# Graph message passing by counting matmuls: 384-column segments with a spill zone, no head chunks, one-hots of 32 chunks

## The chip, the cores and the metric

The kernel runs on one core of one Trainium2 chip. The metric is the device time of one execution in microseconds (us), given as the median of repeated executions. Engines are named as in the profile: PE is TensorE's matmuls, PEld its weight loads, DVE is VectorE, ACT is ScalarE, POOL is GpSimd, SP the engine that only issues DMAs. L360 means line 360 of the kernel that the line belongs to; line numbers differ between kernels, so a helper that issues many matmuls has one line (L359 before, L360 after, is the helper that issues counts, heads and clears).

## The reference

```python
N, E, D = 4096, 262144, 256
def reference(nodes, edges_src, edges_dst, w_msg, w_self):
    self_out = nodes @ w_self
    msg = nodes[edges_src] @ w_msg
    agg = np.zeros((N, D)); np.add.at(agg, edges_dst, msg)
    return self_out + agg
```

The kernel never gathers rows. It sorts the 262144 edges, and then builds, for each block of 128 source nodes and each segment of destination nodes, a matrix of counts ("how many edges go from this source to that destination"). The messages of a segment are then count matrix times Y, where Y = nodes @ w_msg. The counts are made by TensorE: a chunk of 128 sorted edges becomes two one-hot matrices, e_oh (edge x source within the block) and d_oh (edge x destination, relative to a base, 96 wide), and one matmul of the two adds the counts of the chunk to a PSUM bank at an address read from a register.

## The kernel before

The sort is the same in both kernels. After it come 2048 chunks. A run is one (segment, source block) pair: 8 segments of 512 destinations x 32 blocks = 256 runs of about 8 chunks. Each run has its own PSUM bank in a ring of six. The parts that matter (cut):

```python
SEGW, W, SL, RING, MARG, LAG, NRUN = 512, 96, 16, 6, 10, 14, 256

def onehots(src, rel, tag):                  # two VectorE instructions for SL = 16 chunks
    for nm, val, wid in (("e", src, P), ("d", rel, W)):
        o = ohp.tile([P, SL // 2, wid, 2], BF16, ...)
        tt(out=o[:], in0=val...to_broadcast(shp), in1=jrow..., op=ALU.is_equal)

def head_mm(r, he, hd_):                     # opens the bank of run r
    after = [evac_of[r - RING]] if r >= RING else []
    count_mm(ring[:, b:b + W], he, hd_, r % SL, True, after)

def evac(r):                                 # ACT copies the finished bank to SBUF as bf16
    ins = nc.scalar.copy(out=at[:], in_=ring[:, b:b + SEGW]).ins

def apply_run(r):                            # counts x Y, accumulated over the 32 blocks
    for t in range(SEGW // P):
        nc.tensor.matmul(out=out_ps[:, t, :], lhsT=at[:, t * P:(t + 1) * P], rhs=Y[:, b, :], ...)
    # ... after the last block: ACT copies out_ps to o_sb, a DMA stores it

for c in range(NCOL):
    if c % SL == 0:
        e, d = onehots(slo_b[:, sl_], rel_b[:, sl_], "c")
        # ... one-hots of 16 head chunks when due
    for r in range(NRUN):
        if max(8 * r - MARG, 0) == c:
            head_mm(r, *heads[r // SL])
    # ... address of the chunk from a register
    count_mm(ring[:, bass.ds(off, W)], e, d, ci, False)
    # ... evac(nev) and, LAG chunks later, apply_run
```

A chunk that runs over the end of a segment is counted twice: once for the segment that it starts in, and once as the "head chunk" of the next run. The head matmul also opens the bank. To build the one-hots of the heads the kernel must first find the chunks: sorted keys go to DRAM, a count locates the chunk, an indirect DMA fetches it, a transpose turns it.

## Time and profile before

| | before |
|---|---|
| time, median of 3 runs | 798.29 us |
| DVE busy | 717.2 of 796.2 us |
| sort, until the minima k are reduced | 0 to 473 us |
| counting loop | 501.9 us (first matmul) to the end |

The busy row of the page (engine, busy us, share of the span, instructions):

```profile
PE 353.0 (44%) x3906; PEld 300.8 (38%) x3906; DVE 717.2 (90%) x859; ACT 215.9 (27%) x375; POOL 18.6 (2%) x32
```

A share of the whole span mixes the stages. The table of busy time by window separates them; its columns are the window, its length, and busy us (with the number of instructions) of PE, PEld, DVE, ACT and POOL, then the granted TensorE clock, the DMA share and GB/s:

```profile
20.00:480.00 460.00, 108.53 (x512) 87.70 (x512) 419.43 (x531) 50.56 (x96) 7.35 (x6) 0.77 0.08 18
480.00:500.00 20.00, 0.89 (x2) 0.36 (x2) 7.66 (x25) 4.19 (x4) 2.06 (x2) 0.50 0.05 17
600.00:700.00 100.00, 82.87 (x1168) 72.63 (x1166) 100.00 (x101) 54.43 (x94) 0.00 (x0) 0.98 0.05 18
```

In the loop DVE is busy 100 of 100 us. In the window before it, 480 to 500 us, nearly everything stands still, on the way to the head chunks. The timeline of DVE there, with one line of ACT (start, busy us, engine, line, operation, count, and in brackets the idle time before and what ended it):

```profile
484.04 0.95 DVE L343 TENSOR_TENSOR d_oh<-rel_b,jrow 128x1536 bf16<-128x1536 bf16 x1
485.36 0.19 ACT L292 ACTIVATION_READ_ACCUMULATOR junk<-gball,thr 128x1 f32 x1
492.42 0.28 DVE L484 TENSOR_REDUCE bsum<-brow 1x1 f32<-1x128 f32 x1 [7.42 <-DMA brow<-fd]
492.80 0.15 DVE L296 TENSOR_SCALAR cnt<-cnt 128x2 f32<-128x2 f32 x1
496.76 0.29 DVE L314 CAST hs_i<-xt_ps 128x128 int32<-128x128 f32 x1 [3.61 <-PE xt_ps L313]
499.43 1.23 DVE L343 TENSOR_TENSOR e_oh<-hsl,jrow 128x2048 bf16<-128x2048 bf16 x1
```

The first ordinary d_oh is built at 484 us; the loop gets going at 499 us, when the head chunks have come.

How fast is each engine inside the loop? DVE, two one-hot instructions per 16 chunks:

```profile
655.77 1.22 DVE L343 TENSOR_TENSOR e_oh<-slo_b,jrow 128x2048 bf16<-128x2048 bf16 x1
656.90 0.95 DVE L343 TENSOR_TENSOR d_oh<-rel_b,jrow 128x1536 bf16<-128x1536 bf16 x1
657.77 1.22 DVE L343 TENSOR_TENSOR e_oh<-slo_b,jrow 128x2048 bf16<-128x2048 bf16 x1
```

From start to start a pair takes 2.0 us, although the two durations add up to 2.17: they overlap a little, so starts are the right thing to count. PE, in a stretch where it has caught a backlog and does not wait:

```profile
655.48 0.55 PE L359 MATMUL ring<-d_oh,e_oh 128*128 128x96 bf16 x9
655.88 0.60 PE L401 MATMUL out_ps<-Y,at 128*128 128x256 bf16 x4
656.31 0.56 PE L359 MATMUL ring<-d_oh,e_oh 128*128 128x96 bf16 x9
656.70 0.60 PE L401 MATMUL out_ps<-Y,at 128*128 128x256 bf16 x4
```

Nine counts (8 chunks and a head) start 0.40 us before the four applies, which start 0.43 us before the next counts: 44 ns per count, 108 to 109 per apply, 0.83 us per run. An estimate from the Trainium skill comes close: "TensorE: Matmul & The Clock Gate", section Back-to-back issue gap, gives N/2.4 + 2.5 ns for an isolated warm matmul of N columns, from which I estimate 42.5 ns for 96 and 109 for 256. (That section also says that in a stream with weight loads the spacing differs, about 81 ns at N = 128; this trace does not show that.) So PE needs 256 x 0.83 = 212 us where DVE needs 144 pairs x 2.005 = 289 us (128 of chunks, 16 of heads), and the waits agree that PE waits for DVE:

```profile
PE ring L359 <- DVE d_oh L343: 41.3, 84, 4.0
PE out_ps L396 <- ACT o_sb L408: 5.4, 7, 0.8
```

(waited for: us in total, times, longest).

### The profile page before, as it was taken

To read this page: it belongs to the slowest core of one execution; us is meant where nothing else is said; L and a number is where in the kernel's file an instruction comes from. 1 tells how busy PE (TensorE), PEld (TensorE's weight loads), DVE (VectorE), ACT (ScalarE), POOL (GpSimd) and SP (SyncE) were. 2 spreads that over 40 slices of the span, in tenths; PEclk is the share of its full clock that TensorE was granted. 3 is DMA by queue.
4 is the path that set the end of the run, shared out by engine and by line. 5 is a ranking of instruction groups with operands and counts; after the bars stand their busy time and mean duration, and the time that the engine had idled before them with its cause. 6 is when DMAs were issued, how large, how long until landed. Compare 5 with 4: busy or idle time off the path is not lost. (4 is left out here: it accounts for less than half of the span.)

```text
span 796.2 us, 10040 instructions
## 1 busy us (share of the span) xinstructions
PE 353.0 (44%) x3906; PEld 300.8 (38%) x3906; DVE 717.2 (90%) x859; ACT 215.9 (27%) x375; POOL 18.6 (2%) x32
## 2 busy tenths in 40 slices
PE   0013232003232222332212130788888988878886
PEld 0000000002232222332212130667776877767775
DVE  1999999998989888888898973999999999999994
ACT  1001111001111111111101032345555555545554
POOL 4300000000000000000000001000000000000000
PEclk9999999998666655556656655799999999999999
DMA  6741110000000000000000011000000000000000
GB/s 224 105 118 26 25 26 17 0 0 0 1 0 0 1 0 0 0 0 1 0 0 0 0 60 56 1 2 28 2 28 28 2 28 3 27 2 28 2 28 29
DMA packets 25210, 17.91 MB, mean 22 GB/s; under 512 B 11557, under 2 KB 24358, under 8 KB 24390
## 3 DMA queue, kind: packets, MB, share of 16 engines
q1 hardware_dynamic: 19862, 11.59, 4.8%
q0 software_dynamic: 4720, 2.49, 2.3%
q10 hardware_dynamic: 578, 3.16, 1.0%
q8 instruction: 32, 0.52, 0.3%
q14 instruction: 18, 0.15, 0.1%
HBM read 10.12 MB, written 7.37 MB: 22 GB/s over the span
## 5 line engine op out<-in xcount | busy, mean ns | idle before, releaser
L578 DVE TENSOR_TENSOR XA<-XA 128x1024 f32<-128x1024 f32 (+1 forms) x294 | 262.1, 939 | 16.1 <-ACT XA L559 11.3
L375 ACT CAST at<-ring 128x512 bf16<-128x512 f32 x256 | 149.8, 586 | 146.2 <-PE ring L359 146.0
L359 PE MATMUL ring<-d_oh,e_oh 128*128 128x96 bf16 x2304 | 148.0, 208 | 42.7 <-DVE d_oh L343 41.3
L578 DVE TENSOR_TENSOR XB<-XB 128x256 f32<-128x256 f32 (+1 forms) x196 | 139.9, 764 | 19.9 <-ACT XB L559 16.6
L359 PEld LDWEIGHTS <-e_oh 128*128 128x128 bf16 x2304 | 132.8, 99 | 64.2 <-issue 45.4
L343 DVE TENSOR_TENSOR e_oh<-slo_b,jrow 128x2048 bf16<-128x2048 bf16 x128 | 155.9, 1218 | 0.0
L401 PE MATMUL out_ps<-Y,at 128*128 128x256 bf16 x1024 | 155.9, 275 | 0.0
L343 DVE TENSOR_TENSOR d_oh<-rel_b,jrow 128x1536 bf16<-128x1536 bf16 x128 | 121.7, 951 | 0.0
L556 PE MATMUL tp_sw<-sid,XA 128*128 128x128 f32 x224 | 41.7, 372 | 138.6 <-DVE XA L578 138.6
L556 PEld LDWEIGHTS tp_sw<-sid,XA 128*128 128x128 f32 x224 | 40.6, 285 | 139.8 <-issue 139.8
L556 PE MATMUL tp_sw<-ident,XB 128*128 128x128 f32 x224 | 41.6, 371 | 115.7 <-DVE XB L578 115.7
L401 PEld LDWEIGHTS <-at 128*128 128x128 bf16 x1024 | 87.1, 98 | 7.8 <-ACT at L375 0.6
L556 PEld LDWEIGHTS tp_sw<-ident,XB 128*128 128x128 f32 x224 | 40.4, 284 | 116.8 <-issue 116.8
L207 PE MATMUL y_ps<-wcat,XT 128*128 128x256 bf16 x64 | 25.2, 394 | 107.9 <-DMA XT<-nodes_bf_dram 107.9
L559 ACT COPY XB<-tp_sw 128x512 f32<-128x512 f32 x28 | 16.4, 585 | 164.2 <-PE tp_sw L556 164.2
L207 PEld LDWEIGHTS <-XT 128*128 128x128 bf16 x64 | 6.7, 104 | 126.2 <-DMA XT<-nodes_bf_dram 126.2
L559 ACT COPY XA<-tp_sw 128x512 f32<-128x512 f32 x28 | 16.3, 586 | 138.2 <-PE tp_sw L556 138.2
L211 ACT CAST Y<-y_ps 128x256 bf16<-128x256 f32 x32 | 11.9, 372 | 104.0 <-PE y_ps L207 104.0
L343 DVE TENSOR_TENSOR e_oh<-hsl,jrow 128x2048 bf16<-128x2048 bf16 x16 | 19.5, 1219 | 0.0
L343 DVE TENSOR_TENSOR d_oh<-hrel,jrow 128x1536 bf16<-128x1536 bf16 x16 | 15.2, 951 | 0.0
L308 POOL DMA_INDIRECT xh<-xs_dram,cidx x2 | 2.1, 1028 | 466.4 <-DVE cidx L299 466.1
L313 PE MATMUL xt_ps<-ident,xh 128*128 128x128 f32 x2 | 0.9, 447 | 26.3 <-DMA xh<-xs_dram,cidx 26.3
(87 smaller groups left out, 91.9 us busy)
## 6 DMA issues: line engine op xcount, KB each, us to landing
out_dram<-o_sb SPq DMA_DIRECT2D x16, 256.0 KB, 2.3
s<-in_edges_src_dram ACTq DMA_DIRECT2D x2, 1024.0 KB, 12.5
d<-in_edges_dst_dram SPq DMA_DIRECT2D x2, 1024.0 KB, 10.2
nodes_bf<-in_nodes_dram POOLq DMA_DIRECT2D x1, 2048.0 KB, 16.1
nodes_bf_dram<-nodes_bf SPq DMA_DIRECT2D x1, 2048.0 KB, 9.0
XT<-nodes_bf_dram SPq DMA_TRANSPOSE x64, 2.4
xs_dram<-XA ACTq DMA_DIRECT2D x1, 1024.0 KB
gball<-gd SPq DMA_DIRECT2D x1, 1024.0 KB
```

What stands on the lines that cost most here:

```text
L207: nc.tensor.matmul(out=y_ps[:], lhsT=XT[:, k, t * P:(t + 1) * P], rhs=wcat[:, 2 + k, :], start=(k == 0), stop=(k == 1),)
L211: nc.scalar.copy(out=Y[:, t, :], in_=y_ps[:])
L308: nc.gpsimd.indirect_dma_start(out=xh[:], out_offset=None, in_=xs_dram[:, :], in_offset=bass.IndirectOffsetOnAxis(ap=cidx[:, h:h + 1], axi ...
L313: nc.tensor.transpose(xt_ps[:, 0:P], xh[:], ident[:])
L343: tt(out=o[:], in0=val.rearrange("p (g i) -> p g i", i=2).unsqueeze(2).to_broadcast(shp), in1=jrow[:, 0:wid, :].unsqueeze(1).to_broadcast( ...
L359: mm = nc.tensor.matmul(out=ap, lhsT=e[:, ci // 2, :, ci % 2], rhs=d[:, ci // 2, :, ci % 2], start=start, stop=True, skip_group_check=True ...
L375: ins = nc.scalar.copy(out=at[:], in_=ring[:, b:b + SEGW]).ins
L401: nc.tensor.matmul(out=out_ps[:, t, :], lhsT=at[:, t * P:(t + 1) * P], rhs=Y[:, b, :], start=False, stop=(b == T - 1), skip_group_check=True,)
L556: nc.tensor.matmul(out=tp[:, k * P:(k + 1) * P], lhsT=src[:, c], rhs=rhs[:], start=True, stop=True)
L559: nc.scalar.copy(out=dst[:, q * 512:(q + 1) * 512], in_=tp[:])
L578: nc.vector.tensor_tensor(out=d4[:, :, t, :], in0=s4[:, :, 0, :], in1=hi, op=op)
```

## The change

The intent is to take work from DVE. Segments become 384 columns wide, but keep a bank of 512: a chunk that runs over the end of its segment writes on into a spill zone of 96 columns, and the next run adds that zone with one more apply. So there are no head chunks, no head chain, no head one-hots. One-hots are built 32 chunks at a time. The price: 320 runs of 384 and 32 of 256 columns (352 instead of 256), an additional apply per run, and, as no head matmul opens the bank any more, two clears: matmuls of zeros that open the bank and write zeros over its first 96 columns and its spill zone. (They are needed because, as the Trainium skill says in "PSUM — Partial Sum Buffer", section The four PSUM rules, opening a bank clears the marks of what was written, not the data; columns that no count writes would keep old data.) The core of the diff:

```diff
-SEGW = 512
-SL = 16
-MARG = 10
-LAG = 14
-NRUN = 256
+BW = 512
+SW = 384
+NB = 32
+NBIG = 320
+NRUN = 352
+MARG = 9
+LAG = 12
...
     # keys: segment of 384 instead of a shift by 9
+        nc.vector.scalar_tensor_tensor(out=cut, in0=seg, scalar=29.5, in1=blk, op0=ALU.is_gt, op1=ALU.mult)
+        tss(out=seg, in_=seg, scalar=43, op=ALU.mult)
+        tss(out=seg, in_=seg, scalar=7, op=ALU.logical_shift_right)
-        for v, i in ((dlo, 1), (dhi, 2), (shi, 3)):
+        for v, i in ((dlo, 1), (cut, 4), (seg, 2), (blk, 3)):
...
-    # the head chain: Sign/accumulate, indirect DMA, transposes, hsl, hrel
...
+    sizes = [8, 8, 16] + [32] * ((NCOL - 64) // 32) + [16, 8, 8]
+            o = ohp.tile([P, 16, wid, 2], BF16, name=nm + "_oh", tag=nm, bufs=4)
...
+    zer = ohp.tile([P, 2, P], BF16, name="zer")
+    nc.gpsimd.memset(zer[:], 0.0)
...
+    def clear(r):
+        b = (r % RING) * BW
+        w = width(r)
+        after = [evac_of[r - RING]] if r >= RING else []
+        ap = ring[:, b:b + BW]
+        lo = ap[:, 0:W]
+        hi = ap[:, w:w + W]
+        count_mm(lo, zer[0:1, 0, :], zer[0:1, 1, 0:W], True, after)
+        count_mm(hi, zer[0:1, 0, :], zer[0:1, 1, 0:W], False, after)
...
-    def head_mm(r, he, hd_):
...
     def apply_run(r):
+        if r > 0:
+            w = width(r - 1)
+            m = P if w == SW else W
+            nc.tensor.matmul(
+                out=out_ps[0:m, 0, :], lhsT=at_of.pop(r - 1)[:, w:w + m], rhs=Y[:, b, :],
+                start=False, stop=False, skip_group_check=True,
+            )
```

More of the change, by code (lines that the diff above doesn't have):

```diff
@@ L18 @@
 ACTF = mybir.ActivationFunctionType
-SEGW = 512
+BW = 512
+SW = 384
 W = 96
-SL = 16
+NB = 32
+NBIG = 320
+NRUN = 352
+CBIG = 1920
 RING = 6
-MARG = 10
-LAG = 14
-NRUN = 256
+MARG = 9
+MARG2 = 6
+LAG = 12
 PSUM0 = 0x2000000
@@ L59 @@
     T = N // P
-    NSEG = N // SEGW
     NSTAGE = 18
@@ L70 @@
     nodes_bf_dram = dram.tile([N, D], BF16, name="nodes_bf_dram")
-    xs_dram = dram.tile([NCOL, P], FP32, name="xs_dram")
     kd = dram.tile([1, NCOL + 1], FP32, name="kd")
@@ L75 @@
     fd = dram.tile([1, P], FP32, name="fd")
-    rd = dram.tile([1, NCOL + 64], I32, name="rd")
     ident = const.tile([P, P], FP32, name="ident")
@@ L89 @@
     sgn = const.tile([P, 8], FP32, name="sgn")
-    ksg = const.tile([P, 4], FP32, name="ksg")
+    ksg = const.tile([P, 5], FP32, name="ksg")
     nc.gpsimd.iota(sgi[:], pattern=[[0, 8]], base=0, channel_multiplier=1)
@@ L104 @@
     )
-    for i, m in enumerate((1.0, 128.0, float((1 << 21) - (1 << 16)), float((1 << 16) - P))):
+    for i, m in enumerate((1.0, 128.0, float((SW * (NB - 1)) << 7), float((SW << 7) - P), float(-(1 << 14)))):
         nc.vector.tensor_scalar(
@@ L132 @@
         hi = XB[h][:].bitcast(I32)
-        dhi = hi[:, 0:HC]
-        shi = hi[:, HC:2 * HC]
+        seg = hi[:, 0:HC]
+        blk = hi[:, HC:2 * HC]
         key = XA[0][:, h * HC:(h + 1) * HC]
+        cut = XA[1][:, h * HC:(h + 1) * HC]
         nc.scalar.activation(out=key, in_=slo, func=ACTF.Copy, scale=ksg[:, 0:1])
-        tss(out=dhi, in_=dlo, scalar=9, op=ALU.logical_shift_right)
-        tss(out=shi, in_=slo, scalar=7, op=ALU.logical_shift_right)
-        for v, i in ((dlo, 1), (dhi, 2), (shi, 3)):
+        tss(out=blk, in_=slo, scalar=7, op=ALU.logical_shift_right)
+        tss(out=seg, in_=dlo, scalar=7, op=ALU.logical_shift_right)
+        nc.vector.scalar_tensor_tensor(
+            out=cut, in0=seg, scalar=29.5, in1=blk, op0=ALU.is_gt, op1=ALU.mult
+        )
+        tss(out=seg, in_=seg, scalar=43, op=ALU.mult)
+        tss(out=seg, in_=seg, scalar=7, op=ALU.logical_shift_right)
+        for v, i in ((dlo, 1), (cut, 4), (seg, 2), (blk, 3)):
             nc.vector.scalar_tensor_tensor(
@@ L150 @@
     jrow = const.tile([P, P, 2], BF16, name="jrow")
-    hbase = const.tile([P, NRUN], FP32, name="hbase")
-    thr = const.tile([P, 2], FP32, name="thr")
     lo_c = const.tile([P, G16], I32, name="lo_c")
@@ L160 @@
     nc.gpsimd.tensor_copy(out=jrow[:], in_=jrow_i[:])
-    hb_i = stgn.tile([P, NRUN], I32, name="hb_i")
-    nc.gpsimd.iota(hb_i[:], pattern=[[1, NRUN]], base=0, channel_multiplier=0)
-    nc.gpsimd.tensor_copy(out=hbase[:], in_=hb_i[:])
-    nc.gpsimd.tensor_scalar(
-        out=hbase[:], in0=hbase[:], scalar1=float(SEGW), scalar2=None, op0=ALU.mult
-    )
-    nc.gpsimd.memset(hbase[:, 0:1], float(1 << 17))
-    thr_i = stgn.tile([P, 2], I32, name="thr_i")
-    nc.gpsimd.iota(thr_i[:], pattern=[[P, 2]], base=0, channel_multiplier=1)
@@ L170 @@
-    nc.gpsimd.tensor_copy(out=thr[:], in_=thr_i[:])
-    nc.gpsimd.tensor_scalar(
-        out=thr[:], in0=thr[:], scalar1=float(SEGW), scalar2=-0.5, op0=ALU.mult, op1=ALU.add
-    )
-    c_i = stgn.tile([P, G16], I32, name="c_i")
-    nc.gpsimd.iota(c_i[:], pattern=[[1, G16]], base=-MARG, channel_multiplier=G16)
-    nc.vector.tensor_single_scalar(out=lo_c[:], in_=c_i[:], scalar=3, op=ALU.arith_shift_right)
-    c_j = stgn.tile([P, G16], I32, name="c_j")
-    nc.gpsimd.iota(c_j[:], pattern=[[1, G16]], base=MARG, channel_multiplier=G16)
@@ L179 @@
-    nc.vector.tensor_single_scalar(out=hi_c[:], in_=c_j[:], scalar=3, op=ALU.arith_shift_right)
-    NPER = (NCOL + 64) // 48
-    r_i = stgn.tile([1, NPER * 48], I32, name="r_i")
-    nc.gpsimd.iota(
-        r_i[:].rearrange("p (a b c) -> p a b c", b=RING, c=8),
-        pattern=[[0, NPER], [1, RING], [0, 8]], base=0, channel_multiplier=0,
-    )
-    nc.sync.dma_start(rd[0:1, 0:NPER * 48], r_i[:])
-    lo6 = stgn.tile([P, G16], I32, name="lo6")
-    o6 = 48 - MARG
-    nc.sync.dma_start(lo6[:], rd[0, o6:o6 + NCOL].rearrange("(p g) -> p g", g=G16))
@@ L190, with clamp, muladd @@
-    nc.vector.tensor_tensor(out=lom_c[:], in0=lo_c[:], in1=lo6[:], op=ALU.subtract)
+    c_i = stgn.tile([P, G16], I32, name="c_i")
+    ta = stgn.tile([P, G16], I32, name="ta")
+    tb = stgn.tile([P, G16], I32, name="tb")
+    lo6 = stgn.tile([P, G16], I32, name="lo6")
+    def clamp(out, in_, lo, hi):
+        nc.vector.tensor_scalar(
+            out=out, in0=in_, scalar1=float(lo), scalar2=float(hi), op0=ALU.max, op1=ALU.min
+        )
+    def muladd(out, in_, m, a):
+        nc.vector.tensor_scalar(
+            out=out, in0=in_, scalar1=float(m), scalar2=float(a), op0=ALU.mult, op1=ALU.add
+        )
@@ new lines @@
+    for dst, off, top, off2, top2 in (
+        (lo_c, -MARG, CBIG, -MARG2 - CBIG, NCOL - 1 - CBIG),
+        (hi_c, MARG, CBIG - 1, MARG2 + 4 - CBIG, NCOL - CBIG + 3),
+    ):
+        nc.gpsimd.iota(c_i[:], pattern=[[1, G16]], base=0, channel_multiplier=G16)
+        muladd(ta[:], c_i[:], 1, off)
+        clamp(ta[:], ta[:], 0, top)
+        muladd(ta[:], ta[:], 683, 0)
+        tss(out=ta[:], in_=ta[:], scalar=12, op=ALU.logical_shift_right)
+        muladd(tb[:], c_i[:], 1, off2)
+        clamp(tb[:], tb[:], 0, top2)
+        tss(out=tb[:], in_=tb[:], scalar=2, op=ALU.logical_shift_right)
+        tt(out=dst[:], in0=ta[:], in1=tb[:], op=ALU.add)
@@ L192 @@
+    muladd(lo6[:], lo_c[:], 683, 0)
+    tss(out=lo6[:], in_=lo6[:], scalar=12, op=ALU.logical_shift_right)
+    muladd(lom_c[:], lo6[:], RING, 0)
     nodes_bf = stgn.tile([P, T, D], BF16, name="nodes_bf")
@@ L231 @@
     gn = meta.tile([P, G16], I32, name="gn")
+    qa = meta.tile([P, G16], I32, name="qa")
+    qb = meta.tile([P, G16], I32, name="qb")
     dl = meta.tile([P, G16], I32, name="dl")
-    ex = meta.tile([P, G16], I32, name="ex")
     gb = meta.tile([P, G16], FP32, name="gb")
@@ L239 @@
     poffs = meta.tile([1, NCOL], I32, name="poffs")
-    junk = meta.tile([P, NCOL], BF16, name="junk")
-    cnt = meta.tile([P, 2], FP32, name="cnt")
-    cidx = meta.tile([P, 2], I32, name="cidx")
-    nc.scalar.dma_start(xs_dram.rearrange("(p g) l -> p (g l)", g=G16), srt[:])
     nc.vector.tensor_copy(out=k16i[:], in_=k16[:])
     tss(out=gi[:], in_=k16i[:], scalar=7, op=ALU.logical_shift_right)
-    tss(out=dl[:], in_=gi[:], scalar=SEGW - 1, op=ALU.bitwise_and)
-    nc.vector.tensor_scalar(
-        out=ex[:], in0=dl[:], scalar1=float(W - SEGW), scalar2=0.0, op0=ALU.add, op1=ALU.max
-    )
-    tt(out=gb[:], in0=gi[:], in1=ex[:], op=ALU.subtract)
+    nc.vector.tensor_copy(out=gb[:], in_=gi[:])
     nc.sync.dma_start(gd[0, :].rearrange("(p g) -> p g", g=G16), gb[:])
     nc.sync.dma_start(gball[:], gd[0:1, :].broadcast_to([P, NCOL]))
-    tss(out=rho[:], in_=gi[:], scalar=9, op=ALU.logical_shift_right)
+    tss(out=qa[:], in_=gi[:], scalar=7, op=ALU.logical_shift_right)
+    clamp(qb[:], qa[:], 3 * NBIG, 1 << 16)
+    clamp(qa[:], qa[:], 0, 3 * NBIG)
+    muladd(qa[:], qa[:], 683, 0)
+    tss(out=qa[:], in_=qa[:], scalar=11, op=ALU.logical_shift_right)
+    muladd(qb[:], qb[:], 1, -3 * NBIG)
+    tss(out=qb[:], in_=qb[:], scalar=1, op=ALU.logical_shift_right)
+    tt(out=rho[:], in0=qa[:], in1=qb[:], op=ALU.add)
+    nc.vector.scalar_tensor_tensor(
+        out=dl[:], in0=qa[:], scalar=float(-SW), in1=gi[:], op0=ALU.mult, op1=ALU.add
+    )
+    nc.vector.scalar_tensor_tensor(
+        out=dl[:], in0=qb[:], scalar=-256.0, in1=dl[:], op0=ALU.mult, op1=ALU.add
+    )
     tt(out=rhoc[:], in0=rho[:], in1=lo_c[:], op=ALU.max)
@@ L258 @@
     nc.vector.tensor_scalar(
-        out=wr[:], in0=sl[:], scalar1=float(RING), scalar2=float(-RING * SEGW),
+        out=wr[:], in0=sl[:], scalar1=float(RING), scalar2=float(-RING * BW),
         op0=ALU.is_ge, op1=ALU.mult,
@@ L262 @@
     nc.vector.scalar_tensor_tensor(
-        out=wr[:], in0=sl[:], scalar=float(SEGW), in1=wr[:], op0=ALU.mult, op1=ALU.add
+        out=wr[:], in0=sl[:], scalar=float(BW), in1=wr[:], op0=ALU.mult, op1=ALU.add
     )
-    tt(out=dl[:], in0=dl[:], in1=ex[:], op=ALU.subtract)
     tt(out=poff[:], in0=wr[:], in1=dl[:], op=ALU.add)
@@ L288 @@
         tss(out=ki[:, s], in_=ki[:, s], scalar=7, op=ALU.logical_shift_right)
-    for h in range(2):
-        nc.scalar.activation(
-            out=junk[:], in_=gball[:], func=ACTF.Sign, bias=thr[:, h:h + 1], scale=-1.0,
-            accum_out=cnt[:, h:h + 1],
-        )
-    nc.vector.tensor_scalar(
-        out=cnt[:], in0=cnt[:], scalar1=0.5, scalar2=float(NCOL // 2 - 1), op0=ALU.mult, op1=ALU.add
-    )
-    nc.vector.tensor_scalar(
-        out=cidx[:], in0=cnt[:], scalar1=0.0, scalar2=None, op0=ALU.max
-    )
-    hs_i = meta.tile([P, NRUN], I32, name="hs_i")
-    hd_i = meta.tile([P, NRUN], I32, name="hd_i")
-    hsl = meta.tile([P, NRUN], BF16, name="hsl")
-    hrel = meta.tile([P, NRUN], BF16, name="hrel")
-    for h in range(2):
-        xh = meta.tile([P, P], FP32, name=f"xh{h}")
-        nc.gpsimd.indirect_dma_start(
-            out=xh[:], out_offset=None, in_=xs_dram[:, :],
-            in_offset=bass.IndirectOffsetOnAxis(ap=cidx[:, h:h + 1], axis=0),
-        )
-        xt_ps = psum_sort.tile([P, 512], FP32, name="xt_ps", tag="tp", bufs=4)
-        nc.tensor.transpose(xt_ps[:, 0:P], xh[:], ident[:])
-        nc.vector.tensor_copy(out=hs_i[:, h * P:(h + 1) * P], in_=xt_ps[:, 0:P])
-    tss(out=hd_i[:], in_=hs_i[:], scalar=7, op=ALU.logical_shift_right)
-    tss(out=hs_i[:], in_=hs_i[:], scalar=P - 1, op=ALU.bitwise_and)
-    nc.vector.tensor_copy(out=hsl[:], in_=hs_i[:])
-    tt(out=hrel[:], in0=hd_i[:], in1=hbase[:], op=ALU.subtract)
     psum_sort.release()
@@ L330, with onehots @@
     psum2 = tc.alloc_tile_pool(name="psum2", bufs=1, space=bass.MemoryType.PSUM)
-    ring = psum2.tile([P, RING * SEGW], FP32, name="ring")
-    out_ps = psum2.tile([P, SEGW // P, D], FP32, name="out_ps")
+    ring = psum2.tile([P, RING * BW], FP32, name="ring")
+    out_ps = psum2.tile([P, 4, D], FP32, name="out_ps")
     ohp = tc.alloc_tile_pool(name="onehot", bufs=1)
-    def onehots(src, rel, tag):
+    sizes = [8, 8, 16] + [32] * ((NCOL - 64) // 32) + [16, 8, 8]
+    assert sum(sizes) == NCOL
+    def onehots(c, n):
         res = []
-        for nm, val, wid in (("e", src, P), ("d", rel, W)):
-            o = ohp.tile(
-                [P, SL // 2, wid, 2], BF16, name=nm + "_oh", tag=nm + tag,
-                bufs=8 if tag == "c" else 2,
-            )
-            shp = [P, SL // 2, wid, 2]
-            tt(
-                out=o[:],
-                in0=val.rearrange("p (g i) -> p g i", i=2).unsqueeze(2).to_broadcast(shp),
+        for nm, val, wid in (("e", slo_b, P), ("d", rel_b, W)):
+            o = ohp.tile([P, 16, wid, 2], BF16, name=nm + "_oh", tag=nm, bufs=4)
+            shp = [P, n // 2, wid, 2]
+            tt(
+                out=o[:, 0:n // 2],
+                in0=val[:, c:c + n].rearrange("p (g i) -> p g i", i=2).unsqueeze(2).to_broadcast(shp),
                 in1=jrow[:, 0:wid, :].unsqueeze(1).to_broadcast(shp),
@@ L350, in onehots, with seg_of, width, marg @@
         return res
+    zer = ohp.tile([P, 2, P], BF16, name="zer")
+    nc.gpsimd.memset(zer[:], 0.0)
+    NAT = 6
+    ats = [ohp.tile([P, BW], BF16, name=f"at{i}") for i in range(NAT)]
+    for at in ats:
+        nc.gpsimd.memset(at[:], 0.0)
+    def seg_of(r):
+        return divmod(r, NB)
+    def width(r):
+        return SW if r < NBIG else N - SW * (NBIG // NB)
+    def marg(r):
+        return MARG if r < NBIG else MARG2
+    def first(r):
+        return 6 * r if r < NBIG else CBIG + 4 * (r - NBIG)
     DEP = mybir.DependencyInfo(mybir.DependencyClass.Sync, mybir.DependencyReason.DATA)
@@ L355, with count_mm @@
     last_mm = [None]
-    out_v = out.rearrange("(s t p) f -> s p t f", t=SEGW // P, p=P)
-    def count_mm(ap, e, d, ci, start, after=()):
+    def count_mm(ap, lhsT, rhs, start, after=()):
         mm = nc.tensor.matmul(
-            out=ap, lhsT=e[:, ci // 2, :, ci % 2], rhs=d[:, ci // 2, :, ci % 2], start=start, stop=True,
-            skip_group_check=True,
+            out=ap, lhsT=lhsT, rhs=rhs, start=start, stop=True, skip_group_check=True,
         ).ins
@@ L370, in count_mm @@
         return mm
+    def clear(r):
[7 more added lines that the diff above has]
+        count_mm(hi, zer[0:1, 0, :], zer[0:1, 1, 0:W], False, after)
     def evac(r):
-        at = ohp.tile([P, SEGW], BF16, name="at", tag="at", bufs=4)
-        b = (r % RING) * SEGW
-        ins = nc.scalar.copy(out=at[:], in_=ring[:, b:b + SEGW]).ins
+        at = ats[r % NAT]
+        b = (r % RING) * BW
+        n = width(r) + W
+        ins = nc.scalar.copy(out=at[:, 0:n], in_=ring[:, b:b + n]).ins
         tc.declare_no_dep(
@@ L382, in evac @@
         at_of[r] = at
-    def head_mm(r, he, hd_):
-        b = (r % RING) * SEGW
-        after = [evac_of[r - RING]] if r >= RING else []
-        count_mm(ring[:, b:b + W], he, hd_, r % SL, True, after)
     def apply_run(r):
-        s, b = divmod(r, T)
-        at = at_of.pop(r)
+        s, b = seg_of(r)
+        nt = width(r) // P
+        at = at_of[r]
         if b == 0:
-            for t in range(SEGW // P):
+            for t in range(nt):
                 for k in range(2):
-                    c0 = s * SEGW + t * P
+                    c0 = s * SW + t * P
                     nc.tensor.matmul(
@@ L399, in apply_run @@
                     )
-        for t in range(SEGW // P):
+        if r > 0:
[4 more added lines that the diff above has]
+                start=False, stop=False, skip_group_check=True,
+            )
+        for t in range(nt):
             nc.tensor.matmul(
                 out=out_ps[:, t, :], lhsT=at[:, t * P:(t + 1) * P], rhs=Y[:, b, :],
-                start=False, stop=(b == T - 1), skip_group_check=True,
+                start=False, stop=(b == NB - 1), skip_group_check=True,
@@ L404, in apply_run @@
             )
-        if b == T - 1:
-            o_sb = ohp.tile([P, SEGW // P, D], FP32, name="o_sb", tag="o_sb", bufs=2)
-            for t in range(0, SEGW // P, 2):
-                nc.scalar.copy(out=o_sb[:, t:t + 2, :], in_=out_ps[:, t:t + 2, :])
-                nc.sync.dma_start(out_v[s, :, t:t + 2, :], o_sb[:, t:t + 2, :])
+        if b == NB - 1:
+            o_sb = ohp.tile([P, 3, D], FP32, name="o_sb", tag="o_sb", bufs=2)
+            ov = out[s * SW:s * SW + nt * P, :].rearrange("(t p) f -> p t f", p=P)
+            for t0, t1 in ((0, 2), (2, 3)):
+                if t0 < nt:
+                    nc.scalar.copy(out=o_sb[:, t0:t1, :], in_=out_ps[:, t0:t1, :])
+                    nc.sync.dma_start(ov[:, t0:t1, :], o_sb[:, t0:t1, :])
@@ L411 @@
     with tc.manual_schedule():
-        heads = {}
         todo = []
         regs = []
-        nhead = 0
+        ncl = 0
         nev = 0
-        for c in range(NCOL):
-            ci = c % SL
-            if ci == 0:
-                sl_ = slice(c, c + SL)
-                e, d = onehots(slo_b[:, sl_], rel_b[:, sl_], "c")
-                r1 = (c + SL + MARG) // 8
-                while nhead * SL <= min(r1, NRUN - 1):
-                    hsl_ = slice(nhead * SL, (nhead + 1) * SL)
-                    heads[nhead] = onehots(hsl[:, hsl_], hrel[:, hsl_], "h")
-                    nhead += 1
-            for r in range(NRUN):
-                if max(8 * r - MARG, 0) == c:
-                    head_mm(r, *heads[r // SL])
+        starts = {}
@@ L430 @@
+        c = 0
+        for n in sizes:
+            starts[c] = n
+            c += n
+        for c in range(NCOL):
+            if c in starts:
+                c0 = c
+                e, d = onehots(c, starts[c])
+            ci = c - c0
+            while ncl < NRUN and first(ncl) - marg(ncl) <= c:
+                clear(ncl)
+                ncl += 1
             if c % 8 == 0:
@@ L433 @@
             addr = nc.tensor.snap(
-                regs[c % 8], donate=True, min_val=PSUM0, max_val=PSUM0 + 4 * (RING * SEGW - W)
+                regs[c % 8], donate=True, min_val=PSUM0, max_val=PSUM0 + 4 * (RING * BW - W)
             ).with_bounds(
-                min_val=PSUM0, max_val=PSUM0 + 4 * (RING * SEGW - W),
+                min_val=PSUM0, max_val=PSUM0 + 4 * (RING * BW - W),
                 guaranteed_mod_val=0, out_of_modulus=4,
@@ L439 @@
             off = (addr - PSUM0) // 4
-            count_mm(ring[:, bass.ds(off, W)], e, d, ci, False)
-            while nev < NRUN and (8 * nev + 7 + MARG <= c or c == NCOL - 1):
+            count_mm(
+                ring[:, bass.ds(off, W)], e[:, ci // 2, :, ci % 2], d[:, ci // 2, :, ci % 2], False
+            )
+            while nev < NRUN and (first(nev + 1) - 1 + marg(nev) <= c or c == NCOL - 1):
                 evac(nev)
@@ L450 @@
     v = meta.tile([P, G16], FP32, name="v")
-    hh = meta.tile([P, G16], FP32, name="hh")
     bcol = meta.tile([P, 1], FP32, name="bcol")
@@ L460 @@
     tt(out=bad[:], in0=rho[:], in1=rhoc[:], op=ALU.not_equal)
-    nc.vector.tensor_scalar(
-        out=hh[:], in0=rho[:], scalar1=float(SEGW), scalar2=float(SEGW), op0=ALU.mult, op1=ALU.add
-    )
-    nc.vector.scalar_tensor_tensor(
-        out=v[:], in0=gn[:], scalar=1.0, in1=hh[:], op0=ALU.add, op1=ALU.min
-    )
-    tt(out=v[:], in0=v[:], in1=gb[:], op=ALU.subtract)
-    nc.vector.scalar_tensor_tensor(
-        out=bad[:], in0=v[:], scalar=float(W), in1=bad[:], op0=ALU.is_gt, op1=ALU.add
-    )
-    tt(out=v[:], in0=gn[:], in1=hh[:], op=ALU.subtract)
+    tt(out=v[:], in0=gn[:], in1=gb[:], op=ALU.subtract)
     nc.vector.scalar_tensor_tensor(
@@ L474 @@
     )
-    tt(out=v[:], in0=kn[:], in1=k16[:], op=ALU.is_le)
-    tt(out=bad[:], in0=bad[:], in1=v[:], op=ALU.add)
     nc.vector.scalar_tensor_tensor(
```

## The prediction

> **What bounds the kernel now.** The busy table shows VectorE (DVE) at 717 of 796 us. Busy time by window splits this: 20 to 480 us is the sort (DVE 419 of 460), 500 to 786 us the counting loop, DVE always busy. The timeline of the loop shows one pair of one-hots (16 chunks, 1218 + 951 ns) every 2.005 us; 144 pairs (128 of chunks, 16 of heads) make 289 us. TensorE (PE) needs less: where it is not waiting, the timeline repeats 9 count matmuls and 4 applies every 0.83 us, so 44 ns per count, 109 ns per apply, 212 us for 256 runs; the waits list 41 us of PE waiting for d_oh. From 484.0 to 499.4 us DVE is nearly idle: the head chunks come by a chain through DRAM.
>
> **What the change removes.** The head chain: d_oh can start at about 484 instead of waiting until 499 (15 to 17 us, all on the chain). The 16 head pairs, and half of the instructions: the start-to-start times of 1.135 us (2048 elements) and 0.87 us (1536) give 0.52 ns per element and 68 ns per instruction, so 68 pairs take 248 us instead of 289. The r_i iota, with which DVE collided (3.7 us).
>
> **What it adds.** Key building: per half two tensor-scalar ops (about 0.65 us) and two scalar-tensor-tensor ops (1.23 us) more and some 20 tiny constant ops (0.2 us); part fills DVE idle time at 11 to 20 us. I expect the sort to start 4 to 5 us later. PE: 352 runs, each 2 clears, 6 (late 4) counts, 3 (late 2) applies and a spill apply. With 44 and 109 ns: 320 x 0.785 + 32 x 0.59 + 7 for the self matmuls = 277 us, more than DVE's 248. The loop's bottleneck moves to PE. Segment ends go from 7 to 10, each with some 0.8 us waiting for o_sb (5.4 us for 7 now), no longer hidden: 8 us. ACT: 352 evictions of about 0.56 us (586 ns for 512 columns, 372 for 256): not limiting.
>
> **Sum.** PE starts at 484.4 + 4.5 = 489, +277, +8 at segment ends, +3 for a cold clock and the first large one-hots: 777; +7 for the last eviction, copy and output DMA: 784.
> Uncertain: the clears contract over one row, all other matmuls over 128. The Trainium skill ("TensorEngine Tiling (Array Packing)", Key Properties) says that changing the tiling mode drains TensorE; no run here shows it. If the clears run in 32-row tiling, each run has two switches. A count's 208 ns less its 40 ns of streaming bounds a drain at some 170 ns, so this costs 0 to 120 us in all. I allow 11 us on average (30 ns per run): 795 us, 8 in 10 between 777 and 850. Faster by over 2%: 0.2; within 2%: 0.5; slower: 0.3.
>
> **What would show it.** Right: DVE idle 10% or more in the loop, one-hot pairs of 32 in 3.87 us, PE no longer waiting for d_oh but continuous, a run every 0.785 us without drains; first count near 489 us. A drain would show as gaps around the clears (a tile other than 128*128 in their group), runs of 0.9 us or more.
>
> **What would make it wrong.** Drains of over 100 ns per switch (over 850); clears waiting for evictions in the ring of six; sort start delayed by 10 us; or clears that overlap almost free (below 777).

## The result and the profile after

| | before | after |
|---|---|---|
| time, median | 798.28 us (4 runs) | 854.62 us (4 runs) |
| ratio | | 1.0706 (95% interval 1.0688 to 1.0724) |
| span of the profiled run | 796.2 us | 852.9 us |
| first count matmul | 501.9 us | 489.3 us |
| from there to the end | 294.3 us | 363.6 us |

The change is 7% slower. The last two rows are from the timelines of the two profiled runs: the loop starts 12.6 us earlier and takes 69.3 us longer. The busy row and the loop of the kernel after:

```profile
PE 464.4 (54%) x4703; PEld 332.5 (39%) x4703; DVE 688.0 (81%) x724; ACT 254.5 (30%) x472; POOL 20.2 (2%) x29
```

```profile
600.00:700.00 100.00, 98.57 (x1183) 67.91 (x1182) 71.67 (x37) 56.03 (x104) 0.00 (x0) 1.00 0.04 14
```

DVE fell from 100 to 72 us in these 100, PE rose from 83 to 99. The waits have turned round: it is DVE now that waits, for PE to free a one-hot buffer, and the weight loads of line 360 idle 71.5 us, 0.21 us at a time:

```profile
DVE e_oh L326 <- PE ring L360: 94.4, 56, 5.9
PEld L360 <- issue: 71.5, 339, 0.3
PE out_ps L403 <- ACT o_sb L424: 5.2, 10, 0.9
```

The DVE part went as meant. The one-hot pairs, where they do not wait, start 3.87 us apart for 32 chunks (1.94 us per 16, instead of 2.0):

```profile
490.03 2.29 DVE L326 TENSOR_TENSOR e_oh<-slo_b,jrow 128x4096 bf16<-128x4096 bf16 x1
492.23 1.75 DVE L326 TENSOR_TENSOR d_oh<-rel_b,jrow 128x3072 bf16<-128x3072 bf16 x1
493.90 2.29 DVE L326 TENSOR_TENSOR e_oh<-slo_b,jrow 128x4096 bf16<-128x4096 bf16 x1
```

Here is one whole run of PE:

```profile
642.00 0.25 PE L360 MATMUL ring<-zer 1*128 1x96 bf16 x2
642.19 0.43 PE L360 MATMUL ring<-d_oh,e_oh 128*128 128x96 bf16 x6
642.46 0.27 PE L410 MATMUL out_ps<-Y,at 128*128 128x256 bf16 x1
642.57 0.49 PE L415 MATMUL out_ps<-Y,at 128*128 128x256 bf16 x3
642.99 0.25 PE L360 MATMUL ring<-zer 1*128 1x96 bf16 x2
```

It takes 0.99 us. Go through it with 44 ns per count-sized matmul and 109 per apply: two clears should take 0.09, they take 0.19; six counts 0.26, they take 0.27; the spill apply 0.11, it takes 0.11; three applies 0.33, they take 0.42. Some 0.10 us is missing on the way out of the clears and 0.09 on the way into them, none anywhere else. Together this is 0.205 us per run over the 0.785 us expected, and 352 x 0.205 = 72 us.

Note also what the busy numbers do not say. "PE busy 98.57 of 100" looks like a saturated engine, yet a fifth of it (0.205 of 0.99 us) is the time missing around the clears: a matmul's recorded duration (208 ns for a count) is far longer than the 44 ns until the next one starts, so it covers the gap. The Trainium skill warns of this in "Trainium Kernel Development and Optimization", section Performance Expectations: matmul busy time is a bad measure, the busy share of weight loads a good one. This trace agrees: PEld is busy 67.9 of 100 us here, less than the 72.6 of before, with PE at 99.

### The profile page after: what moved, and what is told of

Same layout as the page of the kernel before. It is cut to its first block, busy times and chain, and to the rows that moved or that the text cites. A ratio compares the mean times of both kernels' runs of the same rounds, so it can differ in the third digit from the quotient of the medians.

```text
span 852.9 us, 11638 instructions
## 1 busy us (share of the span) xinstructions
PE 464.4 (54%) x4703; PEld 332.5 (39%) x4703; DVE 688.0 (81%) x724; ACT 254.5 (30%) x472; POOL 20.2 (2%) x29
## 4 chain that ended last, share of the span: by engine, by line
PE 50%; DVE 43%; ACT 3%; DMA 2%; issue 1%; ACTq 0%; DVEq 0%; SPq 0%
DVE XA L582 27%; PE ring L360 22%; PE out_ps L415 13%; DVE XB L582 13%; PE tp_sw L560 9%; PE out_ps L410 4%; DMA s<-in_edges_src_dram 2%; DVE XA L147 1%; PE out_ps L403 1%; ACT o_sb L424 1%; ACT XA L563 1%; DMA gball<-gd 1%; ACT XB L563 0%; ACT ki L293 0%; DVE rel_b L310 0%
## 5 line engine op out<-in xcount | busy, mean ns | idle before, releaser
L582 DVE TENSOR_TENSOR XA<-XA 128x1024 f32<-128x1024 f32 (+1 forms) x294 | 262.2, 939 | 17.8 <-ACT XA L563 13.5
L386 ACT CAST at<-ring 128x480 bf16<-128x480 f32 (+1 forms) x352 | 193.3, 550 | 167.9 <-PE ring L360 167.8
L326 DVE TENSOR_TENSOR e_oh<-slo_b,jrow 128x4096 bf16<-128x4096 bf16 (+2 forms) x68 | 147.2, 2165 | 95.5 <-PE ring L360 94.4
L415 PE MATMUL out_ps<-Y,at 128*128 128x256 bf16 x1024 | 169.0, 273 | 0.0
L360 PEld LDWEIGHTS <-e_oh 128*128 128x128 bf16 x2048 | 101.0, 98 | 37.5 <-issue 9.1
L326 DVE TENSOR_TENSOR d_oh<-rel_b,jrow 128x3072 bf16<-128x3072 bf16 (+2 forms) x68 | 112.7, 1657 | 0.0
L415 PEld LDWEIGHTS <-at 128*128 128x128 bf16 x1024 | 99.3, 97 | 8.3
L410 PE MATMUL out_ps<-Y,at 128*128 128x256 bf16 (+1 forms) x351 | 95.1, 271 | 0.0
L360 PE MATMUL ring<-zer 1*128 1x96 bf16 x704 | 89.8, 207 | 3.9 <-POOL zer L336 3.9
L360 PEld LDWEIGHTS <-zer 1*128 1x128 bf16 x704 | 38.4, 92 | 76.8 <-issue 71.5
L410 PEld LDWEIGHTS <-at 128*128 128x128 bf16 (+1 forms) x351 | 34.6, 99 | 0.2
```

Of the source, the lines that this page charges most:

```text
L326: tt(out=o[:, 0:n // 2], in0=val[:, c:c + n].rearrange("p (g i) -> p g i", i=2).unsqueeze(2).to_broadcast(shp), in1=jrow[:, 0:wid, :].unsq ...
L360: mm = nc.tensor.matmul(out=ap, lhsT=lhsT, rhs=rhs, start=start, stop=True, skip_group_check=True,).ins
L386: ins = nc.scalar.copy(out=at[:, 0:n], in_=ring[:, b:b + n]).ins
L410: nc.tensor.matmul(out=out_ps[0:m, 0, :], lhsT=at_of.pop(r - 1)[:, w:w + m], rhs=Y[:, b, :], start=False, stop=False, skip_group_check=True,)
L582: nc.vector.tensor_tensor(out=d4[:, :, t, :], in0=s4[:, :, 0, :], in1=hi, op=op)
```

## The experiments

**Theories.** A, drain: the one-row clears run in another tiling of the array than the 128-row matmuls around them, and each change of tiling, into the clears and out of them, empties TensorE. The Trainium skill says in "TensorEngine Tiling (Array Packing)", section Key Properties: "Changing tiling mode (not just tile) drains the TensorE", without a figure. B, per instruction: a one-row matmul is slow in itself (its weight load, say). C, eviction: the clears wait for ACT to free the bank, six runs back.

### Clears over 128 rows (k128)

```diff
-        count_mm(lo, zer[0:1, 0, :], zer[0:1, 1, 0:W], True, after)
-        count_mm(hi, zer[0:1, 0, :], zer[0:1, 1, 0:W], False, after)
+        count_mm(lo, zer[0:128, 0, :], zer[0:128, 1, 0:W], True, after)
+        count_mm(hi, zer[0:128, 0, :], zer[0:128, 1, 0:W], False, after)
```

> The clears contract over 128 rows of zeros instead of one; nothing else changes. Drain theory (each change between the tiling of the one-row clears and that of the 128-row matmuls empties TensorE, about 0.10 us, two per run): a run falls from 0.99 to about 0.79 us, 352 x 0.205 = 72 us come back, time about 783 us (780 to 788). Eviction theory (the clears wait for the bank to be evicted): the waits are the same, so 850 to 856 us. Power or clock theory: no change or slower.

Measured: 783.28 us (4 runs), ratio to before 0.9812 (0.979 to 0.9835). The results are correct, as in all the experiments. One run of PE:

```profile
700.16 0.25 PE L360 MATMUL ring<-zer 128*128 128x96 bf16 x2
700.24 0.42 PE L360 MATMUL ring<-d_oh,e_oh 128*128 128x96 bf16 x6
700.51 0.27 PE L410 MATMUL out_ps<-Y,at 128*128 128x256 bf16 x1
700.62 0.49 PE L415 MATMUL out_ps<-Y,at 128*128 128x256 bf16 x3
700.94 0.25 PE L360 MATMUL ring<-zer 128*128 128x96 bf16 x2
```

The clears now take 0.08 us instead of 0.19 and the three applies 0.32 instead of 0.42; the run takes 0.78 us. Everything else in the kernel, the waits for banks included, is the same, so theory C falls: 71.3 us came back from a change of the number of rows alone. A difference of clock is no rival: the granted clock is 1.00 from 600 to 700 us in both. (Against the kernel before this is 1.9% faster; whether it is 2%, the interval leaves open.) The window shows how the two busy measures differ: PE is as busy as in the kernel after (97.95), but PEld went from 67.91 to 91.72.

```profile
600.00:700.00 100.00, 97.95 (x1484) 91.72 (x1482) 90.33 (x47) 70.05 (x129) 0.00 (x0) 1.00 0.04 14
```

### 64 rows and 65 rows (k64, k65)

```diff
+        count_mm(lo, zer[0:64, 0, :], zer[0:64, 1, 0:W], True, after)      # k64
+        count_mm(lo, zer[0:65, 0, :], zer[0:65, 1, 0:W], True, after)      # k65; hi likewise
```

> Clears over 64 rows. Drain theory, with tilings of 32, 64 and 128 rows: still another tiling, so about 855 us, as with one row (850 to 860). If only the number of rows mattered (narrow loads are slow), it should lie between one row (855) and 128 rows (about 783), near 820.

> Clears over 65 rows, one more than in k64. Drain theory: 65 rows need the 128-row tiling, so no change of tiling and the same as 128 rows, about 783 us (780 to 788). A smooth dependence on rows would give the same as k64 within 1 us.

Measured: 853.53 us with 64 rows, 787.51 us with 65 (2 runs each). First k64, then k65, the clears and what follows:

```profile
699.85 0.26 PE L360 MATMUL ring<-zer 64*128 64x96 bf16 x2
700.04 0.44 PE L360 MATMUL ring<-d_oh,e_oh 128*128 128x96 bf16 x6
```

```profile
700.08 0.25 PE L360 MATMUL ring<-zer 65*128 65x96 bf16 x2
700.16 0.43 PE L360 MATMUL ring<-d_oh,e_oh 128*128 128x96 bf16 x6
```

One row more makes the kernel 66 us faster. No smooth cost of a row can do that; a tiling with a border at 64 can. The page named above gives 64 and 32 rows as the row tilings, in its section When to Use Tiling ("contract dim ≤ 64"); the border at 64 agrees, and whether one row is tiled as 32 or as 64 rows, no run shows. (Of the 5.9 us between the profiled runs of 65 and 128 rows, 3.4 were there before the first count: 490.7 against 487.4 us. Another 1.7 are a slightly slower loop: a segment of 32 runs takes 26.74 us instead of 26.57, and the clears' starts are 47 ns apart instead of 42. Why, is open.)

### The second clear moved behind a count (sep)

```diff
-        count_mm(hi, zer[0:1, 0, :], zer[0:1, 1, 0:W], False, after)
+        late.append((hi, after))
 ...
     count_mm(ring[:, bass.ds(off, W)], e[...], d[...], False)
+            while late:
+                hi, after = late.pop(0)
+                count_mm(hi, zer[0:1, 0, :], zer[0:1, 1, 0:W], False, after)
```

> One-row clears as in the change, but the second clear of each run is issued after the next count matmul instead of directly behind the first: same instructions, four changes of tiling per run instead of two. Drain theory: another 352 x 0.2 = 72 us, about 925 us (915 to 935). If each one-row instruction costs its 0.1 us by itself, the same 855 us.

Measured: 926.52 us (2 runs), 71.9 us more than the kernel after.

```profile
700.08 0.21 PE L360 MATMUL ring<-zer 1*128 1x96 bf16 x1
700.23 0.22 PE L360 MATMUL ring<-d_oh,e_oh 128*128 128x96 bf16 x1
700.38 0.21 PE L360 MATMUL ring<-zer 1*128 1x96 bf16 x1
700.52 0.39 PE L360 MATMUL ring<-d_oh,e_oh 128*128 128x96 bf16 x5
```

The instructions are the same as in the kernel after, only their order differs, so theory B falls. Each single clear or count between two changes now takes 0.15 us instead of 0.044. The dose is straight: 0, 2 and 4 changes per run cost 783.3, 854.6 and 926.5 us, so 71 to 72 us per 704 changes, 0.10 us each.

What happens inside TensorE at a change is not measured; "drain" is the page's word for it. The weight loads of the clears, first in the kernel after and then in k128, show one difference:

```profile
642.99 0.11 PEld L360 LDWEIGHTS <-zer 1*128 1x128 bf16 x2 [0.21 <-issue]
700.83 0.21 PEld L360 LDWEIGHTS <-zer 128*128 128x128 bf16 x2
```

In k128 the load starts 0.11 us before its matmul (700.94), while the last apply runs; in the kernel after it starts together with its matmul (642.99). So the 0.10 us can be an emptying of the array, or a weight load (0.09 to 0.10 us) that may no longer run ahead of its matmul across a change. The runs do not separate the two. They show what a change costs, and that it is the change that costs it.

### The same drains in the kernel before (before_drain)

If a drain is TensorE time, it should hurt less where TensorE is not the limit. The kernel before got one one-row matmul of zeros behind each head matmul (the diff leaves out the zero tile and the declarations of dependences):

```diff
         count_mm(ring[:, b:b + W], he, hd_, r % SL, True, after)
+        mm = nc.tensor.matmul(
+            out=ring[:, b:b + W], lhsT=zer[0:1, 0, :], rhs=zer[0:1, 1, 0:W], start=False, stop=True,
+            skip_group_check=True,
+        ).ins
```

> The kernel before, with one more matmul per run: one row of zeros added to the columns that the head matmul just wrote (it changes no value). Drain theory: two changes of tiling per run, so TensorE needs 0.83 + 0.04 + 0.20 = 1.07 us per run, still under the 1.13 us that VectorE takes: the drains cost 52 us of TensorE time but under 1% of the kernel's, 798 to 806 us. If drains delayed the kernel wherever they stand, it would be near 850.

Measured: 810.87 us against 799.35 us of before in the same rounds, ratio 1.0142 (1.0125 to 1.0158): 11.5 us, not the 62 us (256 x 0.24) that TensorE spends more, but also more than the 7 us that I expected at most. The windows of the end, and PE's only wait for d_oh (4.0 us), show why:

```profile
780.00:790.00 10.00, 9.70 (x127) 7.87 (x125) 7.82 (x8) 5.08 (x10) 0.00 (x0) 1.00 0.01 2
790.00:800.00 10.00, 9.86 (x128) 8.09 (x128) 0.00 (x0) 5.08 (x10) 0.00 (x0) 1.00 0.00 0
800.00:811.00 11.00, 2.94 (x32) 1.93 (x28) 0.00 (x0) 3.19 (x6) 0.00 (x0) 0.74 0.17 52
```

```profile
PE ring L359 <- DVE d_oh L343: 4.0, 1, 4.0
```

DVE is done at 787.8 us, almost as before (786.1). But PE, which waited 41.3 us for d_oh before, now waits for it once, before the first count, and works on for 15 us after DVE's end (before: 3 us). From its first matmul (503.6 us) to its last (803.0) it takes 299 us, where DVE needs 289: the drains have made PE the limit here too. The 1.07 us per run was right (the zero matmuls of two runs that do not halt start at 603.28 and 604.36 us, 1.08 apart), but my sum left out the self matmuls (7 us), the segment ends, the cold start and some 18 short halts of PE between 0.2 and 1 us (7 us in all), whose cause I did not find. So this run shows that drains cost less where TensorE has time to spare, and not that they are free there.

### One-hots of 16 in k128, and of 32 in the kernel before (k128_oh16, b32)

These take the parts of the change apart.

```diff
 # k128_oh16
-    sizes = [8, 8, 16] + [32] * ((NCOL - 64) // 32) + [16, 8, 8]
+    sizes = [8, 8] + [16] * ((NCOL - 32) // 16) + [8, 8]
-            o = ohp.tile([P, 16, wid, 2], BF16, name=nm + "_oh", tag=nm, bufs=4)
+            o = ohp.tile([P, 8, wid, 2], BF16, name=nm + "_oh", tag=nm, bufs=8)
 # b32, from the kernel before
-SL = 16
+SL = 32
-                bufs=8 if tag == "c" else 2,
+                bufs=4 if tag == "c" else 2,
```

> Clears over 128 rows, but one-hots built 16 chunks at a time as in the kernel before (8 buffers of 16 instead of 4 of 32). VectorE then needs 128 pairs of 2.005 us, 257 us instead of 248, still less than the 277 us of TensorE. If the loop is bound by TensorE once the drains are gone: within 2 us of the 783 us of k128. If VectorE still binds: about 9 us more, 792.

> The kernel before with only one part of the change: one-hots built 32 at a time (heads too). VectorE binds that loop; 144 instructions of 68 ns go, 10 us: about 789 us (786 to 793), ratio 0.987. If the larger one-hots make TensorE wait longer at the start or in the ring, less is won (793 to 799).

Measured: k128_oh16 784.02 us, ratio to before 0.9807 (k128: 0.9812 in its rounds), so the larger one-hots are worth nothing there; b32 787.48 us, ratio 0.986 (0.9842 to 0.9878), so where DVE is the limit they are worth the 10 us of instructions that they save. Saving DVE time pays in the kernel before and not in k128, as the limit has moved. This edit of two lines (SL = 32 and half as many buffers) alone wins two thirds to three quarters of what the whole reworked kernel wins once its clears are mended.

### The spill added elsewhere (k128_pool, k128_dve)

With the drains gone, PE is the limit by 277 to 248 us, and 351 spill applies make up 38 us of it. The zone can instead be added to the next run's evicted tile. Both edits below come on top of the clears over 128 rows. On GpSimd:

```diff
+        if r > 0:                                   # in evac(r), after the copy
+            w = width(r - 1)
+            nc.gpsimd.tensor_tensor(
+                out=at[:, 0:W], in0=at[:, 0:W], in1=at_of[r - 1][:, w:w + W], op=ALU.add
+            )
-        if r > 0:                                   # in apply_run(r)
-            # ... the spill matmul
-    NAT = 6
+    NAT = 8
-LAG = 12
+LAG = 18
```

> Clears over 128 rows; the spill zone is added to the first 96 columns of the next run's evicted tile by the idle GpSimd (352 adds of 128x96 bf16) instead of by 351 matmuls of 109 ns. TensorE falls from 277 to 239 us, VectorE stays at 248 and becomes the limit again: about 755 us (750 to 765) if the adds take under 0.5 us each and do not slow VectorE. If they share a port with the one-hot instructions, these get longer than 3.87 us per pair and the time stays at 770 to 790; if the adds are slower than a run (0.7 us) TensorE waits for them and it is above 790.

Measured: 896.8 us, ratio 1.1225 (1.1196 to 1.1253): much worse. The group of the adds, and who waited in the loop:

```profile
L396 POOL TENSOR_TENSOR at<-at,at x351: 353/363/13489, 493.2 to 887.2; 128x96 bf16<-128x96 bf16 x176
```

```profile
PE out_ps L413 <- POOL at L396: 75.3, 77, 9.0
POOL at L396 <- ACT at L386: 67.3, 71, 9.6
```

The columns of the first are minimum, median and maximum ns of one: half of the adds take 0.36 us, but one took 13.5 us, and the mean is 0.913 us. PE waits for them, and d_oh became longer too (1909 ns from 1749). The Trainium skill says in "SBUF — State Buffer" (Terms, shared port pair) that VectorE and GpSimd arbitrate for one pair of ports, held for a whole instruction, and that the loser blocks fully. The trace agrees in detail: all 117 adds that took over 1 us began while a one-hot instruction ran, and each ended 0.22 us after the end of one; the adds that began while none ran took 0.35 to 0.37 us. The add of 13.5 us (from 493.16 us) began in a d_oh and lasted through six more one-hot instructions without a gap between them, so the wait need not end with the instruction that was running. No run here measured the port by itself.

On VectorE, in every third run, with the one-hots issued two blocks ahead:

```diff
+        if r % 3 == 1:                              # in evac(r)
+            w = width(r - 1)
+            tt(out=at[:, 0:W], in0=at[:, 0:W], in1=at_of[r - 1][:, w:w + W], op=ALU.add)
-        if r > 0:                                   # in apply_run(r)
+        if r % 3 != 1 and r > 0:
-    NAT = 6
+    NAT = 14
-LAG = 12
+LAG = 40
...
-                e, d = onehots(c, starts[c])
+                while ahead and len(built) < 3:
+                    c1 = ahead.pop(0)
+                    built.append(onehots(c1, starts[c1]))
+                e, d = built.pop(0)
```

> Clears over 128 rows; in every third run the spill is added to the next run's tile by VectorE (117 adds of 128x96 bf16, about 0.13 us each) instead of by a matmul; one-hots are issued two blocks ahead and the applies 40 chunks behind, so that the adds need not wait. TensorE falls by 13 us to 264, VectorE rises by about 15 to 263: about 772 us (766 to 779) if both stay busy. If VectorE, in order, waits for the evictions and TensorE for the adds, nothing is won or it is slower (783 to 830).

Measured: 777.42 us (4 runs) against 799.35 us, ratio 0.973 (0.9708 to 0.9752): the fastest of all, and the only one clearly over 2% faster than the kernel before. In the loop PE and DVE are both nearly full; the adds took 0.20 us, not 0.13. The one-hots issued ahead were not run by themselves, but they can hardly be what won: in k128 PE waits in the loop for o_sb alone (7.1 us), not for one-hots.

```profile
600.00:700.00 100.00, 96.57 (x1479) 90.12 (x1476) 96.79 (x90) 72.31 (x133) 0.00 (x0) 1.00 0.06 18
```

| kernel | changes of tiling per run | median us |
|---|---|---|
| before | 0 | 798 to 799 |
| after | 2 | 854.62 |
| k128 / k65 | 0 | 783.28 / 787.51 |
| k64 | 2 | 853.53 |
| sep | 4 | 926.52 |
| before_drain | 2 (256 runs) | 810.87 |
| k128_oh16 | 0 | 784.02 |
| b32 | 0 | 787.48 |
| k128_pool | 0 | 896.8 |
| k128_dve | 0 | 777.42 |

## Why the prediction was wrong

The prediction said 795 us, between 777 and 850, most likely within 2%. It was 854.6, 7% slower.

- **The step that failed** is the term for the clears: "I allow 11 us on average (30 ns per run)". The mechanism was named, with the page that states it, and the bounds for it (0 to 120 us) contain the truth. But the size was set near the low end of that range, at 15 ns per change. It is 0.10 us per change, 0.205 us per run, 72 us in all (after against k128: 71.3). With 72 in place of 11 the sum gives 856 us.
- **The sum without that term was right**: 784 us predicted, 783.28 us measured with the clears over 128 rows. That it fits within 1 us is luck: the sum was made in the time of the trace, where k128 took 780.4 us, as the first count came 1.6 us earlier than predicted and the tail after the last matmul took 4.9 us instead of 7. Its parts were nearly right: a run of 0.785 us (0.78), pairs of 32 in 3.87 us (3.87), the first count at 489 us (489.28 after, 487.36 in k128), the sort 4 to 5 us later (its last minimum is ready 4.4 us later: the cast that follows starts at 477.22, before at 472.80), 8 us at ten segment ends (7.1 in k128).
- **"The loop's bottleneck moves to PE"** was right: DVE waits 94 us for PE in the kernel after, and 9 us more of DVE work (k128_oh16) change nothing.
- **"Clears waiting for evictions in the ring of six"**, named as a way to be wrong, did not happen: the waits list nothing of the kind, and k128 kept the same dependencies.
- **What the hedge ignored.** That the clears' shape differs from all others was in the diff, and the page says without a condition that a change of mode drains. Unknown were whether a one-row matmul counts as another mode without being told to, and the size. A count's 208 ns against its 40 ns of streaming (an estimate from the starts: 160 columns more take 65 ns more, so 96 take 39) left room for much more than 15 ns. Half of that bound, per change, would have given 844 us.

## What to carry to other kernels

Before making a matmul smaller along its contraction, look at what stands beside it: a single matmul of few rows (1 and 64 were tested) among 128-row ones costs two drains of about 0.10 us here, each more than twice its own 44 ns, while the full 128 rows of zeros cost nothing more. Group such matmuls or pad them, and look for the gap in the starts of successive matmuls and in the busy share of weight loads, since matmul busy time hides it. And when work moves from the engine at the limit to another, sum up both engines after the move: here TensorE rose to 277 us while VectorE fell to 248 (both are sums of measured steps), so most of the saving was gone before any drain, and moving a part back won more.

## What the Trainium skill lacked or had wrong

- "TensorEngine Tiling (Array Packing)", Key Properties, says that a change of tiling mode drains TensorE, but has no figure. Here one change costs 0.10 us at the full clock: 783.3, 854.6 and 926.5 us with 0, 2 and 4 changes in each of 352 runs.
- The same page, When to Use Tiling, offers 64 and 32 rows as an option for small contractions. It does not say that a matmul with few rows is tiled without being asked to (the kernel names no tiling; that it is tiled is concluded from the border between 64 and 65 rows), nor that one such matmul in a stream of full ones is a loss. 64 rows: 853.5 us; 65 rows: 787.5 us.
- "TensorE: Matmul & The Clock Gate", Back-to-back issue gap, gives about 81 ns as the sustained spacing of load and matmul pairs at N = 128. Here pairs of a 128x128 load and a 96-column matmul start 44 ns apart and those with 256 columns 109 ns, which fits that section's isolated formula instead. (No matmul of 128 columns runs in the loop.)
- "SBUF — State Buffer" says that the pair is held for one instruction and that the loser blocks fully. It does not say that the wait can outlast that instruction under a dense stream of VectorE work: adds with a median of 0.36 us took up to 13.5 us, through seven one-hot instructions in a row, and 0.913 us on average.
